# The causal mask of the mLSTM gates: on GpSimd after the exponential instead of in a matmul before it

## The chip, the cores and the metric

The kernel runs on one core of a Trainium2 chip. The metric is the device time of one execution in microseconds (us). The engines of the core are named PE (TensorE, matmuls; PEld is its weight load), DVE (VectorE), ACT (ScalarE), POOL (GpSimd) and SP (SyncE, here a DMA queue). SBUF is the on-chip memory in which tiles lie, PSUM the banks into which PE writes.

## The reference, cut to what matters

The model is a trunk of two layers over 256 tokens of width 1024. Each layer has a half-step SwiGLU network, a mixer, and a second half-step SwiGLU network, with a normalization before and after each. The mixer projects the tokens, runs differential attention on four heads and an mLSTM on four other heads beside it, and projects both back. The change is in the mLSTM, whose gates make a causal matrix of weights in each chunk:

```
causal = jnp.tril(jnp.ones((CHUNK, CHUNK), dtype=bool))
D = jnp.where(causal, b[..., :, None] - b[..., None, :] + log_i[..., None, :], -jnp.inf)
m_inter = b + m_prev[..., None]
m = jnp.maximum(m_inter, D.max(-1))
w = jnp.exp(D - m[..., None]) * jnp.einsum('bhcjd,bhcsd->bhcjs', q, k)
```

For a query j and a key s of the same chunk the exponential is exp(D - m), at most one where s <= j, and zero where s > j. Everywhere above the diagonal the unmasked exponent can be of any size. The kernel works with chunks of 128 tokens, so that its chunk is one tile of tokens, and keeps the matrix turned round: keys on the 128 partitions, four heads of 128 queries in the 512 columns.

## The kernel before, in words

The weights come from HBM in pieces of 1 MB on SP's queue (`begin_piece`, L281). Each half of a piece is split in two parts for accuracy: ACT rounds it to the PE's fast float32 form (tile wh, L287), DVE subtracts that from the original (wl, L288). A product of the activations xh, xl with such weights is three matmuls of 128x512 (`mm3`, L401 to L403: xh by wh, xh by wl, xl by wh). The feed-forward networks take most of the time and use the same split (L611, L614).

The mixer projects two tiles of 128 tokens (t = 0, 1) through six groups of 512 columns. Its order of work is written by hand: `traverse` lists steps of one `mm3` each, and `AT` (L39) gives for every stage of the rest the step in front of which it stands. PE follows that order exactly; for ACT, DVE and POOL the framework fixes an order when the program is built, from the dependencies, from priorities and from its own estimate of when operands are there. Every engine then runs its queue in that order. The projections go to two PSUM banks in turn (tag pin), and an evacuation on ACT frees them: `rope` (L1056) for queries and keys, `values_ml` (L1151), `output_gate`.

The stages that matter here, by the step in front of which they stand:

- 22, `gate_chain`: the running sums of the gates and their maximum on DVE, in rows (tiles ul and md).
- 24, `conv_input_t(1)`, `conv((2, 3))`, `gate_exps(0)`, `gate_exps(1)` and `roped(0, 0)`. `gate_exps(t)` multiplies ul by md on PE (L997), which spreads u[s] - M[j] over a 128x512 bank, adds the mask in the same bank by a second matmul (L998: the identity by the mask, 0 where allowed and -1e30 elsewhere), and takes the exponential on ACT into the tile eE (the helper `func`, L265).
- 40, `conv((0, 1))`, and 46, `conv_silu`: the causal convolution of the mLSTM's queries and keys, each block one step on ACT (L906) and three on DVE (L909), and its SiLU on ACT (tile qk).
- 34, 43, 57, `roped`: transposes on PE (L878) of the rotated queries and keys of the attention. The rotation itself is four DVE instructions in `rope` (L1057, twice L1062, L1063), made for each token tile when its projection is done.
- 52, `scores` and `intra_weights`: the attention scores, and the product of eE with the mLSTM's scores on DVE (L1048, tile wt).
- 60 and later, `combine`, `normed_ml`, `attend`: here POOL computes reciprocal square roots as powers (`rsqrt`, L416). Besides these, POOL sets memory at the start (L218 to L248) and copies four small gate tiles in each layer (L943).

The mask, the rounded mask and the rounded identity are made once, in `constants_mix` (L201 to L206), in the middle of the first network.

Of the kernel before, what the change touches and what calls it, by code (L numbers as in the profile page):

```python
# [17 lines left out]
F32 = mybir.dt.float32  # L18
F32R = mybir.dt.float32r
AF = mybir.ActivationFunctionType  # L20
ALU = mybir.AluOpType
# [3 lines left out]
P = 128  # L25
# [7 lines left out]
CH = P  # L33
EPS = 1e-6
BIG = -1.0e30
# [23 lines left out]
def _pack(inp):  # L59


    f32 = np.float32
    x = np.asarray(inp["x"])
    w_in, w_out = np.asarray(inp["ffn_w_in"]), np.asarray(inp["ffn_w_out"])
    m_in, m_out = np.asarray(inp["mix_w_in"]), np.asarray(inp["mix_w_out"])
    g = np.asarray(inp["norm_gains"])
    w = np.empty((L * PIECES_LAYER, P, 2048), f32)

    def ffn(at, l, f):
        a = w_in[l, f].reshape(2, 4, P, 2, NC_FF, 256)  # L70
        a = a.transpose(4, 0, 2, 1, 3, 5).reshape(NC_FF, 2, P, 2048)
        b = w_out[l, f].reshape(NC_FF, 2, P, D).transpose(0, 2, 1, 3).reshape(NC_FF, P, 2048)
        order = [a[0, 0], a[0, 1]]
        for c in range(1, NC_FF):
            order += [a[c, 0], a[c, 1], b[c - 1]]
        for piece in order + [b[NC_FF - 1]]:
            w[at] = piece
            at += 1

    for l in range(L):  # L80
        at = l * PIECES_LAYER
        ffn(at, l, 0)
        at += PIECES_FFN
        for n, lo in enumerate(MIX_GROUPS):
            a = m_in[l][:, lo:lo + 512].reshape(2, 4, P, 512).transpose(0, 2, 1, 3)
            w[at + 2 * n:at + 2 * n + 2] = a.reshape(2, P, 2048)
        at += 2 * len(MIX_GROUPS)
        w[at:at + 4] = m_out[l].reshape(4, 2, P, D).transpose(0, 2, 1, 3).reshape(4, P, 2048)
        ffn(at + 4, l, 1)
    for i in range(2):  # L90
        w[i] = w[i].reshape(P, 4, 512).transpose(1, 0, 2).reshape(P, 2048)

    arrays = {
        "x": x.reshape(NT, P, 2, 512).transpose(0, 2, 1, 3),
        "w": w,
        "gpost": g[:, 1::2].reshape(L * 3, D),
        "lam": np.asarray(inp["da_lambda"]).reshape(L, 256),
    }
    arrays = {k: np.ascontiguousarray(v) for k, v in arrays.items()}
    gpre = g[:, 0::2].reshape(L, 3, KT, P).transpose(3, 0, 1, 2).reshape(P, L * 3 * KT)  # L100
    arrays["c0"] = np.concatenate([np.eye(P, dtype=f32), gpre], 1)

    inv = (f32(10000.0) ** (-np.arange(0, 64, 2, dtype=f32) / f32(64))).astype(f32)
    ang = np.arange(S, dtype=f32)[:, None] * inv[None, :]
    cos, sin = np.cos(ang).astype(f32), np.sin(ang).astype(f32)
    rope = np.stack([np.concatenate([cos, cos], 1), np.concatenate([-sin, sin], 1)])
    s = np.arange(P)[:, None]
    j = np.arange(P)[None, :]
    mask = np.where((s // CH == j // CH) & (s <= j), 0.0, BIG).astype(f32)
    first = (np.arange(S) % CH == 0)  # L110
    scan = np.stack([np.where(first, 0.0, 1.0), np.where(first, BIG, 0.0)]).astype(f32)

    def everywhere(v):
        return np.broadcast_to(np.asarray(v).reshape(1, -1), (P, np.asarray(v).size))

    parts = {
        "wg": m_in[:, :, 3072:3080].reshape(L, KT, P, 8).transpose(2, 0, 1, 3),
        "rope": rope.reshape(2, NT, P, 64).transpose(2, 0, 1, 3),
        "convw": np.asarray(inp["ml_conv_w"]).reshape(L, 4, 4, P).transpose(3, 0, 2, 1),
        "convb": np.asarray(inp["ml_conv_b"]).reshape(L, 4, P).transpose(2, 0, 1),  # L120
        "gda": np.asarray(inp["da_subln_g"]).T,
        "gml": np.asarray(inp["ml_norm_g"]).T,
        "gateb": everywhere(inp["ml_gate_b"]),
    }
    arrays["c1"] = np.concatenate([parts[n].reshape(P, -1) for n, _ in C1], 1)
    arrays["mask"] = mask
    arrays["scan"] = np.ascontiguousarray(np.broadcast_to(scan.reshape(1, 512), (100, 512)))
    return arrays


class _Trunk:
# [50 lines left out]
    def constants_mix(self):  # L182
        nc, a = self.nc, self.a
# [11 lines left out]
        for l in range(L):  # L195
# [2 lines left out]
        self.wgc = self.const.tile([P, L, KT, 16], F32R, name="c_wgc")  # L198
        ia = nc.scalar.activation(self.wgc[:, :, :, 0:8], self.wg, AF.Copy)
        iv = nc.vector.tensor_tensor(self.wgc[:, :, :, 8:16], self.wg, self.wgc[:, :, :, 0:8].bitcast(F32), op=ALU.subtract)  # L200
        mraw = self.t2("mraw", (P, P))  # L201
        self.after(nc.sync.dma_start(mraw, a["mask"]), [self.load])
        self.mask = self.const.tile([P, P], F32R, name="c_mask")
        self.identr = self.const.tile([P, P], F32R, name="c_identr")
        nc.scalar.activation(self.mask, mraw, AF.Copy)
        self.after(nc.scalar.activation(self.identr, self.ident, AF.Copy), [ia])  # L206

        lamv = self.t2("lamv", (P, L, 4, 64))
        self.after(nc.sync.dma_start(lamv.rearrange("p l a b -> p l (a b)"), a["lam"].partition_broadcast(P)), [self.load])
# [11 lines left out]
                                     op=ALU.add)  # L221
# [535 lines left out]
class _Mixer:  # L757
# [234 lines left out]
    def gate_exps(self, t):  # L992

        tr = self.tr
        cols = slice(t * P, t * P + P)
        pe = tr.bank_bk()
        self.mm(pe, tr.ul[:, cols], tr.md[:, t].rearrange("p h j -> p (h j)"), start=True, stop=False)  # L997
        self.mm(pe, tr.identr, tr.mask.unsqueeze(1).broadcast_to([P, 4, P]), start=False, stop=True)  # L998
        eE = tr.t2("eE")
        tr.func(eE, pe, AF.Exp)  # L1000
        self.eE.append(eE)

    def gate_decays(self):
# [252 lines left out]
```

## Time and profile before

| what | us |
|---|---|
| median of the runs | 977.39 (977.36 to 977.74) |
| the profiled execution | 979.73 |
| its span | 976.9 |
| busy: PE, DVE, ACT, POOL | 969.4, 710.2, 568.0, 30.1 |
| granted clock of PE, mean | 0.999 |

The profile records one execution. The span runs from the first to the last instruction of the program; the execution's time has 2.8 us more around it. A line of the profile gives the line of the kernel, the engine, the operation, and the tiles as out<-in without their numbers; L265 and L416 are helpers, so there one goes by the tiles. The busy time of PE counts matmuls that overlap, and their ends are modelled. "Idle before" is the time that an engine stood still just before an instruction, with the instruction that ended it.

### The profile page before, as it was taken

The numbers are of one execution on the slowest core, as the hardware profiler recorded it, in microseconds if no ns is written. First come the engines' busy times: TensorE is split into PE (matmuls) and PEld (weight loads), VectorE is DVE, ScalarE is ACT, GpSimd is POOL, SyncE is SP. The second block draws the span as 40 slices with busy tenths as digits, with TensorE's granted clock in tenths as the row PEclk, the third lists the DMA queues.
The fourth block names the chain that finished last, engine by engine and source line by source line (L and its number), as shares of the span: only waits on it lengthen the run. The fifth ranks groups of instructions, "written<-read, shape, count | busy, mean of one in ns | idle before, by whom it ended". The sixth has DMA issues, their size and how long they took to land.

```text
span 976.9 us, 13520 instructions
## 1 busy us (share of the span) xinstructions
PE 969.4 (99%) x5061; PEld 818.1 (84%) x5061; DVE 710.2 (73%) x1178; ACT 568.0 (58%) x1041; POOL 30.1 (3%) x55
## 2 busy tenths in 40 slices
PE   9999999999999999999999999999999999999997
PEld 6888888888788888888888888888888888888886
DVE  6787676689867677767687767676997687776664
ACT  7665554477756565455375545454778475555541
POOL 2000000000020000000000000000001000000000
PEclk9999999999999999999999999999999999999999
DMA  8954545336352845564356456443454256554511
GB/s 296 353 199 174 206 170 198 142 129 225 118 197 92 317 163 182 180 240 183 131 204 233 151 205 221 174 171 114 173 209 172 88 207 239 202 193 173 193 67 43
DMA packets 27647, 178.92 MB, mean 183 GB/s; under 512 B 3034, under 2 KB 4186, under 8 KB 6846
## 3 DMA queue, kind: packets, MB, share of 16 engines
q1 hardware_dynamic: 27006, 177.46, 50.0%
q8 instruction: 39, 0.64, 0.3%
q10 hardware_dynamic: 576, 0.61, 0.2%
q14 instruction: 26, 0.21, 0.1%
HBM read 177.01 MB, written 1.05 MB: 182 GB/s over the span
## 4 chain that ended last, share of the span: by engine, by line
PE 99%; DVE 0%; ACT 0%; POOLq 0%; issue 0%; DVEq 0%; ACTq 0%
PE ptr L611 14%; PE pin L611 14%; PE bk L402 10%; PE bk L403 10%; PE bk L401 10%; PE pin L401 7%; PE pin L403 7%; PE pin L402 7%; PE ptr L614 7%; PE pin L614 7%; PE ptr L878 1%; PE ptr L427 1%; PE bk L1093 1%; PE bk L1131 1%; PE bk L378 0%; PE bk L379 0%
## 5 line engine op out<-in xcount | busy, mean ns | idle before, releaser
L288 DVE TENSOR_TENSOR wl<-wr,wh 128x1024 fp32r<-128x1024 f32 x324 | 388.6, 1222 | 130.3 <-ACT wh L287 128.5
L287 ACT ACTIVATE wh<-wr 128x1024 fp32r<-128x1024 f32 x324 | 332.1, 1053 | 123.8 <-PE ptr L611 57.7
L611 PE MATMUL pin<-both,wh 128*128 128x512 f32 x576 | 157.3, 394 | 0.0
L611 PE MATMUL ptr<-both,wh 128*128 128x512 f32 x576 | 157.0, 394 | 0.0
L402 PE MATMUL bk<-wl,hh 128*128 128x512 f32 x352 | 137.6, 391 | 0.0
L401 PE MATMUL bk<-wh,hh 128*128 128x512 f32 x352 | 137.4, 390 | 0.0
L403 PE MATMUL bk<-wh,hl 128*128 128x512 f32 x352 | 136.8, 391 | 0.0
L401 PE MATMUL pin<-wh,both 128*128 128x512 f32 x304 | 122.3, 403 | 0.0
L402 PE MATMUL pin<-wl,both 128*128 128x512 f32 x304 | 118.9, 392 | 0.0
L403 PE MATMUL pin<-wh,both 128*128 128x512 f32 x304 | 118.7, 391 | 0.0
L611 PEld LDWEIGHTS pin<-both,wh 128*128 128x128 f32 x576 | 100.7, 189 | 14.9
L611 PEld LDWEIGHTS ptr<-both,wh 128*128 128x128 f32 x576 | 98.8, 189 | 13.8
L614 PEld LDWEIGHTS ptr<-both,wl 128*128 128x128 f32 x576 | 88.3, 189 | 12.2
L614 PEld LDWEIGHTS pin<-both,wl 128*128 128x128 f32 x576 | 88.2, 189 | 11.7
L614 PE MATMUL pin<-both,wl 128*128 128x256 f32 x576 | 92.4, 281 | 0.0
L614 PE MATMUL ptr<-both,wl 128*128 128x256 f32 x576 | 91.6, 281 | 0.0
L546 ACT ACTIVATE hh<-su 128x256 fp32r<-128x256 f32 (+1 forms) x96 | 32.1, 355 | 94.4 <-PE bk L402 77.9
L403 PEld LDWEIGHTS bk<-wh,hl 128*128 128x128 f32 x352 | 66.1, 188 | 14.0
L401 PEld LDWEIGHTS bk<-wh,hh 128*128 128x128 f32 x352 | 66.1, 188 | 12.8
L402 PEld LDWEIGHTS bk<-wl,hh 128*128 128x128 f32 x352 | 66.1, 188 | 12.8
L403 PEld LDWEIGHTS pin<-wh,both 128*128 128x128 f32 x304 | 57.1, 188 | 12.4
L401 PEld LDWEIGHTS pin<-wh,both 128*128 128x128 f32 x304 | 57.2, 188 | 11.8 <-issue 0.7
(203 smaller groups left out, 982.9 us busy)
## 6 DMA issues: line engine op xcount, KB each, us to landing
wr<-in_w_dram SPq DMA_DIRECT2D x162, 1024.0 KB, 4.8
gpost<-in_gpost_dram SPq DMA_DIRECT2D x6, 512.0 KB, 5.7
wr<-in_w_dram SPq DMA_DIRECT2D x2, 512.0 KB, 6.0
wr<-in_w_dram SPq DMA_DIRECT2D x3, 256.0 KB, 4.2
x<-in_x_dram SPq DMA_DIRECT2D x3, 256.0 KB, 4.8
out_dram<-x SPq DMA_DIRECT2D x2, 256.0 KB, 2.1
x<-in_x_dram SPq DMA_DIRECT2D x2, 128.0 KB, 3.0
wr<-in_w_dram ACTq DMA_DIRECT2D x1, 256.0 KB, 3.9
```

The source lines that it names most:

```text
L287: ia = nc.scalar.activation(hi, raw[:, j], AF.Copy)
L288: iv = nc.vector.tensor_tensor(lo, raw[:, j], hi.bitcast(F32), op=ALU.subtract)
L401: mm(ps, xh, wh, start=start, stop=False)
L402: mm(ps, xh, wl, start=False, stop=False)
L403: mm(ps, xl, wh, start=False, stop=stop)
L427: nc.tensor.transpose(ptr[:, k, :], x[:, (4 * hf + k) * P:(4 * hf + k + 1) * P], self.ident)
L546: self.nc.scalar.activation(hh, h, AF.Copy)
L611: self.nc.tensor.matmul(b, self.cols(w, k)[0][:, c], both[:, k].rearrange("p i t -> p (i t)"), start=kh == 0 and k == 0, stop=False, skip_ ...
L614: self.nc.tensor.matmul(b[:, 0:NT * P], self.cols(w, k)[1][:, c], both[:, k, 0:NT].rearrange("p i t -> p (i t)"), start=False, stop=kh == ...
L878: self.T(ptr[:, b, :], a[:, b * P:(b + 1) * P], self.tr.ident)
L1093: self.mm(pcs[c][:, h, :], self.qkT[0][rows, h0 + h, t * P:(t + 1) * P], self.qkT[1][rows, h0 + h, 0:nk], start=True, stop=True)
L1131: self.mm(po[:, h, :], self.aT[t][:, kt, h, :], self.vd[:, kt, h * P:(h + 1) * P], start=kt == 0, stop=kt == t)
```

## The change

The mask changes from 0 and -1e30 to 1 and 0. `gate_exps` loses the second matmul. After the exponential, two instructions on POOL work in place on eE: a minimum with one, which bounds what lies above the diagonal, and a product with the mask, repeated over the four heads. The rounded identity and the two rounding copies on ACT go; the mask is loaded straight into its constant tile.

```
@@ in _pack
-    mask = np.where((s // CH == j // CH) & (s <= j), 0.0, BIG).astype(f32)
+    mask = np.where(s <= j, 1.0, 0.0).astype(f32)
@@ in constants_mix
-        mraw = self.t2("mraw", (P, P))
-        self.after(nc.sync.dma_start(mraw, a["mask"]), [self.load])
-        self.mask = self.const.tile([P, P], F32R, name="c_mask")
-        self.identr = self.const.tile([P, P], F32R, name="c_identr")
-        nc.scalar.activation(self.mask, mraw, AF.Copy)
-        self.after(nc.scalar.activation(self.identr, self.ident, AF.Copy), [ia])
+        self.mask = self.const.tile([P, P], F32, name="c_mask")
+        self.after(nc.sync.dma_start(self.mask, a["mask"]), [self.load])
@@ in gate_exps
-        self.mm(pe, tr.ul[:, cols], tr.md[:, t].rearrange("p h j -> p (h j)"), start=True, stop=False)
-        self.mm(pe, tr.identr, tr.mask.unsqueeze(1).broadcast_to([P, 4, P]), start=False, stop=True)
+        self.mm(pe, tr.ul[:, cols], tr.md[:, t].rearrange("p h j -> p (h j)"), start=True, stop=True)
         eE = tr.t2("eE")
         tr.func(eE, pe, AF.Exp)
+        e4 = eE.rearrange("p (h j) -> p h j", h=4)
+        tr.nc.gpsimd.tensor_scalar(eE, eE, 1.0, None, op0=ALU.min)
+        tr.nc.gpsimd.tensor_tensor(e4, e4, tr.mask.unsqueeze(1).broadcast_to([P, 4, P]), op=ALU.mult)
         self.eE.append(eE)
```

## The prediction

> **What bounds the kernel now.** I read the page first: the busy shares and the chain that ended last. Then the waits of TensorE (PE) alone.
>
> ```profile
> PE 969.4 (99%) x5061; PEld 818.1 (84%) x5061; DVE 710.2 (73%) x1178; ACT 568.0 (58%) x1041; POOL 30.1 (3%) x55
> PE 99%; DVE 0%; ACT 0%; POOLq 0%; issue 0%; DVEq 0%; ACTq 0%
> ```
>
> ```profile
> PE bk L390 <- DVE mp L979: 1.2, 1, 1.2
> ```
>
> PE is busy for 99% of the span, the chain is PE from end to end, and the only wait of PE that the trace lists is one of 1.2 us at the very start. So the time is the sum of what PE issues. Two kinds of change count: one that takes instructions off PE, and one that makes PE wait where it never waited. VectorE (DVE) at 73% as an average says nothing yet; it has to be read in the stage that the change touches.
>
> **What a matmul of the mask is worth.** The timeline of PE around the edited lines, second layer (columns: start, busy time, engine, line, operation, tiles), and the group of the removed line over the whole span (last numbers: busy us in total, mean ns of one, idle us before):
>
> ```profile
> 704.50 0.47 PE L997 MATMUL bk<-md,ul 100*128 100x512 f32 x1
> 704.82 0.40 PE L998 MATMUL bk<-c_mask,c_identr 128*128 128x512 f32 x1
> 705.05 0.39 PE L997 MATMUL bk<-md,ul 100*128 100x512 f32 x1
> 705.28 0.40 PE L998 MATMUL bk<-c_mask,c_identr 128*128 128x512 f32 x1
> 705.52 0.60 PE L878 MATMUL ptr<-c,ra 128*128 128x128 f32 x4
> ```
>
> ```profile
> L998 PE MATMUL bk<-c_mask,c_identr 128*128 128x512 f32 x4 | 1.6, 396 | 0.0
> ```
>
> The group says 396 ns each, 1.6 us in all, but matmuls overlap: what one costs is the distance to the next start. L998 starts at 704.82 and 705.28, its followers at 705.05 and 705.52: 0.23 and 0.24, 0.47 us for the two of a layer. Two layers make 0.93 us, 0.1% of the time. Its weight loads lie beside other matmuls and go at nothing. The two ScalarE (ACT) copies of the set-up, L205 and L206, go too; they run once, off PE's chain, and I price them at nothing. The mask's DMA stays. The exponential keeps its size.
>
> **What GpSimd (POOL) is given.** For each of two token tiles in each of two layers, a minimum (one input, 128x512) and a product (two inputs, 128x512). The trace has no arithmetic of that size on POOL. Its nearest rows, with mean ns of one after the bar:
>
> ```profile
> L218 POOL MEMSET g<- 128x512 f32 x1 | 0.5, 524 | 0.0
> L240 POOL MEMSET vx<- 128x1032 f32 x1 | 1.0, 963 | 0.0
> L943 POOL COPY g<-gn 128x16 f32<-128x16 f32 x4 | 0.7, 202 | 14.8 <-DVE gn L941 14.8
> L416 POOL TENSOR_TENSOR rs<-s,c_half 128x1 f32<-128x1 f32 x24 | 13.1, 552 | 767.9 <-DVE s L452 767.9
> ```
>
> The memsets give (963-524)/520 = 0.84 ns per column, the small copy about 0.20 us of fixed cost. The minimum is then an estimated 0.20+0.43 = 0.63 us, and the product, which has to fetch two operands, 0.20+2x0.43 = 1.06 us: 1.69 us a tile, 3.4 us a layer. A lower bound is the plain memset, 0.52 each.
>
> In time POOL has room. The exponentials (ACT timeline, first layer) and the first reader of the masked tile (DVE timeline):
>
> ```profile
> 223.70 0.59 ACT L265 ACTIVATE eE<-bk 128x512 f32<-128x512 f32 x1
> 226.15 0.58 ACT L265 ACTIVATE eE<-bk 128x512 f32<-128x512 f32 x1
> ```
>
> ```profile
> 248.87 0.73 DVE L1048 SCALAR_TENSOR_TENSOR wt<-bk,eE 128x256 f32<-128x256 f32 x2
> ```
>
> The tiles are there at 224.29 and 226.73 and are wanted at 248.87: 22 us for 3.4 us of work. L1048 now waits for POOL instead of ACT; behind it in DVE's queue stand the maxima of the attention scores.
>
> **What POOL does to VectorE.** This is where the sum turns. POOL's powers beside DVE's instructions, first layer, POOL's timeline and then DVE's:
>
> ```profile
> 270.14 1.01 POOL L416 TENSOR_TENSOR rs<-ssm,c_half 128x4 f32<-128x4 f32 x1 [61.91 <-ACT wh L287]
> 271.56 1.01 POOL L416 TENSOR_TENSOR rs<-ssa,c_half 128x4 f32<-128x4 f32 x1 [0.41 <-DVE ssa L1138]
> 273.52 2.09 POOL L416 TENSOR_TENSOR rs<-ssa,c_half 128x4 f32<-128x4 f32 x1 [0.94 <-DVE ssa L1138]
> 278.84 1.28 POOL L416 TENSOR_TENSOR rs<-ssm,c_half 128x4 f32<-128x4 f32 x1 [3.23 <-DVE ssm L1205]
> ```
>
> ```profile
> 270.18 1.23 DVE L288 TENSOR_TENSOR wl<-wr,wh 128x1024 fp32r<-128x1024 f32 x1 [0.19 <-ACT wh L287]
> 273.52 1.23 DVE L288 TENSOR_TENSOR wl<-wr,wh 128x1024 fp32r<-128x1024 f32 x1
> 278.58 0.69 DVE L1189 SCALAR_TENSOR_TENSOR so<-so,hn 128x512 f32<-128x512 f32 x1
> ```
>
> These rows settle two things on the way. POOL's queue is empty until 270.14, so nothing of its own waits behind the new instructions. And the far end of POOL's price: a power of 128x4 takes 1.01 us against 0.55 for 128x1, 0.15 us per column, which would be 79 us for 512. I stay with the memset's pace, since the copy of 16 columns at 0.20 us is nowhere near the power's.
>
> Now the port. The same power takes 1.01 us twice, but 2.09 when L288, a DVE instruction with two SBUF inputs, starts with it, and 1.28 beside L1189, which also has two. Taking 1.01 off the ends 275.61 and 280.12, POOL got going at 274.60 and 279.11; the DVE instructions end at 274.75 and 279.27. So POOL stood still until 0.15 us before their end: the two exclude each other. The trace doesn't show the reverse, DVE held by POOL; beside the power at 270.14, L288 keeps its 1.23 us, though that power reads four columns only. Now DVE in the stretch where the new instructions fall: first the stretches view (columns: window, length, busy time of PE, PEld, DVE, ACT, POOL with counts, granted clock, DMA), then DVE's timeline.
>
> ```profile
> 224.00:237.30 13.30, 13.30 (x64) 11.07 (x63) 13.30 (x26) 12.62 (x17) 0.00 (x0) 1.00 0.62 232
> ```
>
> ```profile
> 224.21 0.68 DVE L1057 TENSOR_TENSOR ra<-rv,c 128x512 f32<-128x512 f32 x1
> 224.81 0.75 DVE L1062 TENSOR_TENSOR rb<-rv,c 128x256 f32<-128x256 f32 x2
> ...
> 227.22 4.44 DVE L909 SCALAR_TENSOR_TENSOR conv<-xpad,c,conv 128x256 f32<-128x256 f32 x11
> ...
> 236.65 0.69 DVE L1063 TENSOR_TENSOR ra<-ra,rb 128x512 f32<-128x512 f32 x1
> ```
>
> DVE is busy for 13.30 of 13.30 us, and each of those instructions (rotation, convolution, weight split) reads two SBUF tensors. So whatever POOL takes from DVE between 224.3 and 236.7 comes out late at 236.65, with nothing to absorb it. Does POOL get in? In back-to-back work DVE's next instruction starts 0.08 us before the end of the one before (224.81 against 224.21+0.68); POOL got going 0.15 us before. It was there first, so I take it that POOL wins at the next boundary and DVE then stands still while POOL reads.
>
> **Who waits for DVE there.** The rotated keys of L1063 are transposed on PE by L878 (PE's timeline, then the second layer's pair from DVE and PE):
>
> ```profile
> 237.83 0.60 PE L878 MATMUL ptr<-c,ra 128*128 128x128 f32 x4
> ```
>
> ```profile
> 718.23 0.69 DVE L1063 TENSOR_TENSOR ra<-ra,rb 128x512 f32<-128x512 f32 x1
> ```
>
> ```profile
> 719.41 0.60 PE L878 MATMUL ptr<-c,ra 128*128 128x128 f32 x4
> ```
>
> L1063 ends at 237.34 and 718.92, the transposes start at 237.83 and 719.41: 0.49 us of slack in both layers. Removing the two L998 brings PE there 0.47 us earlier, while DVE, which is behind, comes no earlier. So the change of a layer is the larger of -0.47 and d-0.49, with d the time that DVE loses: the gain is spent as soon as d reaches 0.49. A second path is nearly as tight:
>
> ```profile
> 233.22 1.06 ACT L265 ACTIVATE qk<-conv 128x1024 f32<-128x1024 f32 x1 [0.28 <-DVE conv L909]
> 234.19 0.67 ACT L1056 ACTIVATE rv<-pin,rs 128x512 f32<-128x512 f32 x1
> ```
>
> ```profile
> 235.78 0.39 PE L401 MATMUL pin<-wh,both 128*128 128x512 f32 x1
> ```
>
> ACT's SiLU waits for the convolution on DVE; behind it in ACT's queue, L1056 empties the bank that PE refills at 235.78 (the second token tile of the values): 234.86 against 235.78, slack 0.92, 0.45 with PE earlier. It would show a stall first; the transposes then add the rest, so the two aren't added up.
>
> **The sum.** d lies between nothing (POOL yields always) and 3.4 us (DVE loses all of POOL's time); without POOL's fixed 0.20 of each instruction, when it reads nothing, 2.6. I take 3.0, between the last two. Each layer then loses 3.0-0.49 = 2.5 us, two lose 5.0. The profiled execution took 979.73 us with a span of 976.9; it would take 984.7 with a span of 981.9. It lies 2.34 above the median of the runs, 977.39; the difference carries over, so the median becomes 982.4.
>
> The Trainium skill bears on two of these places. "SBUF — State Buffer", section "Who interferes with whom", says that a DVE instruction with two SBUF inputs and a GpSimd instruction that reads SBUF hold the shared port against each other, the first for its whole instruction; the trace agrees on DVE holding off POOL (2.09 against 1.01), but the whole instruction is too much for a power of four columns, beside which L288 kept its 1.23. "GPSIMD Engine Reference", section 3.1, gives 4497 ns for an addition of two tensors of 2048 columns and 769 ns for a tight loop over 512: an estimated 1.12+0.77 a tile, so d = 3.8 and a loss of 6.6 instead of 5.0; no row here has either.
>
> **The rivals.** *POOL yields* (not slower): POOL gets no boundary while DVE runs back to back. It works in DVE's pauses before 248.87, and PE keeps its 0.93: 976.5. For it: the trace has no DVE instruction lengthened by POOL. Against it: the 0.15 us by which POOL was first, twice. It decides from d under 0.49. Chance 0.28.
>
> *A partial hold*: POOL stops DVE only while it actually fetches, or DVE reaches the rotation in another order, so that d is between 0.49 and 1.47. Then two layers cost up to 2x(1.47-0.49) = 1.96, which is the 0.2%: 976.5 to 979.3. Chance 0.08.
>
> *The mask comes late*: if POOL computes at the power's pace, the tile isn't ready at 248.87, L1048 stands in DVE's queue and with it the scores. At 79 us an instruction, 316 us a layer less the 24.6 from 224.29 to 248.87: some 580 us more for both. For it only that pow row, against it the copy's. Chance 0.02.
>
> Forecast 0.62: the cases of d from 1.47 to 4.5, that is 979.3 to 985.4.
>
> **How the numbers follow.** 0.2%, 1.95 us, is about what a measurement of this kernel can tell from no change. Slower: 0.62+0.02 = 0.64. Same: the -0.93 of a yielding POOL is within it, and so is the partial hold: 0.28+0.08 = 0.36, of which I set 0.03 aside as faster, for a reordering of DVE that I can't see; on PE there is no more than 0.93 to be had. The range starts at 976.4, so that it holds the yielding POOL, and ends at 985.2, which is d = 4.4: POOL a third slower than the memset's pace makes it. The forecast's own range is 979.3 to 985.2.
>
> **What would show it.** Right: L998 gone; two pairs of POOL instructions of about 0.6 and 1.1 us or longer after each exponential; DVE instructions there that start late or last 0.5 to 1.1 us longer; the waits of PE, empty so far, naming L1063 before L878, or L1056's bank before L401, some 2.5 us a layer; all other stages of the same length. Wrong: PE's waits still empty and the span 0.9 shorter (POOL yields); or the stall elsewhere, at L1048 and the scores (the mask late); or POOL's instructions far from 0.6 and 1.1 without a wait.

## The result and the profile after

The changed kernel takes 989.05 us (median of 4 runs, 988.13 to 990.87) against 977.38 us before: a ratio of 1.012 (95% interval 1.0108 to 1.0132), 11.7 us slower. The forecast was 982.4 us, 5.0 slower. The direction held, and the wait came where it was expected, but it was longer and brought a second cost behind it.

The page of the changed kernel, its busy shares, the granted clock in 40 slices and the chain that ended last (lines move by 4 to 2 against before: L1061 is the old L1063, L874 the old L878, L284 the old L288, L905 the old L909):

```profile
span 989.1 us, 13523 instructions
PE 973.5 (98%) x5057; PEld 820.0 (83%) x5057; DVE 716.1 (72%) x1178; ACT 567.0 (57%) x1039; POOL 43.5 (4%) x63
PEclk9999999998999999999999999999989999999999
PE 94%; DVE 4%; issue 0%; ACT 0%; DMA 0%; POOLq 0%; DVEq 0%; ACTq 0%
```

PE has lost its four matmuls, and DVE has entered the chain with 4%. Two slices of the clock, one in each layer's mixer, show an 8 where all stood at 9. The waits of PE (us in total, times, longest):

```profile
PE ptr L874 <- DVE ra L1061: 8.1, 2, 4.0
```

Twice 4.0 us, at the transposes of the rotated keys, one wait in each layer. PE's timeline of the first layer's place, with the four instructions behind the wait:

```profile
236.55 0.39 PE L399 MATMUL pin<-wh,both 128*128 128x512 f32 x1
240.97 1.09 PE L874 MATMUL ptr<-c,ra 128*128 128x128 f32 x4 [4.03 <-DVE ra L1061]
241.71 0.78 PE L397 MATMUL pin<-wh,both 128*128 128x512 f32 x1
242.28 0.63 PE L398 MATMUL pin<-wl,both 128*128 128x512 f32 x1
242.71 0.63 PE L399 MATMUL pin<-wh,both 128*128 128x512 f32 x1
```

Behind the wait matmuls start 0.43 us apart instead of 0.23. The stretches view shows why (window, length, busy PE, PEld, DVE, ACT, POOL, then the granted clock; the last two columns are DMA):

```profile
241.50:246.50 5.00, 5.00 (x15) 3.99 (x14) 3.56 (x5) 1.65 (x2) 0.00 (x0) 0.51 0.81 295
246.50:252.00 5.50, 5.50 (x42) 4.52 (x42) 2.06 (x4) 2.82 (x4) 0.00 (x0) 1.00 0.15 63
729.50:734.50 5.00, 5.00 (x15) 3.94 (x14) 3.45 (x5) 1.65 (x2) 0.00 (x0) 0.50 0.74 279
```

For about 5 us after the wait PE runs at half its clock, in both layers of the profiled execution. Set against the trace of before, matmul by matmul, the distance of PE's starts changes, behind the start-up, in three places of each layer alone. In the first layer it stands at -0.61 us before the gates (the start-up, which varies from run to run), goes to -1.08 where the mask matmuls are missing, to 3.14 at the transposes and to 5.69 in the half-clock stretch. In the second it goes from 5.69 to 5.23, 9.45 and 12.11. Each layer so loses 4.2 us to the wait and 2.6 to the clock, and gains 0.47: 6.3 to 6.4, twice.

Now the two engines that share the place. POOL's new groups and DVE's timeline, first layer:

```profile
L997 POOL TENSOR_SCALAR eE<-eE 128x512 f32<-128x512 f32 x4 | 8.2, 2056 | 32.4 <-ACT eE L261 32.4
L998 POOL TENSOR_TENSOR eE<-eE,c_mask 128x512 f32<-128x512 f32 x4 | 5.5, 1385 | 0.0
```

```profile
223.61 0.69 DVE L1055 TENSOR_TENSOR ra<-rv,c 128x512 f32<-128x512 f32 x1
224.21 1.17 DVE L1060 TENSOR_TENSOR rb<-rv,c 128x256 f32<-128x256 f32 x2
...
227.45 5.77 DVE L905 SCALAR_TENSOR_TENSOR conv<-xpad,c,conv 128x256 f32<-128x256 f32 x9
...
237.88 2.35 DVE L284 TENSOR_TENSOR wl<-wr,wh 128x1024 fp32r<-128x1024 f32 x2
240.15 0.68 DVE L1061 TENSOR_TENSOR ra<-ra,rb 128x512 f32<-128x512 f32 x1
```

From the first of these instructions to the end of the key rotation DVE took 13.13 us before (224.21 to 237.34); now it takes 17.22 (223.61 to 240.83). Two things are in that. Instructions are longer: the pair of L1060 lasts 1.17 instead of 0.75. And the order is another: ahead of the rotation's last step stand two weight splits in a row, where one stood before:

```profile
235.51 1.22 DVE L288 TENSOR_TENSOR wl<-wr,wh 128x1024 fp32r<-128x1024 f32 x1
```

The framework fixed a new order when the program was built. ACT's queue shows a new order too: both exponentials now stand in a row, ahead of the four convolution steps that stood between them before (223.70 and 226.15 in the prediction):

```profile
223.09 1.08 ACT L261 ACTIVATE eE<-bk 128x512 f32<-128x512 f32 x2
```

That the framework does this because the second exponential is ready one matmul earlier is argued, not shown; for it speaks that e3, which puts the convolution steps back between the two, brings back DVE's order.

### The profile page after: what moved, and what is told of

Read it like the earlier page. It is cut to its first block, busy times and chain, and to the rows that moved or that the text cites. A ratio compares the mean times of both kernels' runs of the same rounds, so it can differ in the third digit from the quotient of the medians.

```text
span 989.1 us, 13523 instructions
## 1 busy us (share of the span) xinstructions
PE 973.5 (98%) x5057; PEld 820.0 (83%) x5057; DVE 716.1 (72%) x1178; ACT 567.0 (57%) x1039; POOL 43.5 (4%) x63
## 4 chain that ended last, share of the span: by engine, by line
PE 94%; DVE 4%; issue 0%; ACT 0%; DMA 0%; POOLq 0%; DVEq 0%; ACTq 0%
PE ptr L607 14%; PE pin L607 13%; PE bk L398 10%; PE bk L399 10%; PE bk L397 10%; PE ptr L610 7%; PE pin L610 7%; PE pin L397 6%; PE pin L398 6%; PE pin L399 6%; DVE wl L284 2%; DVE conv L905 1%; PE ptr L423 1%; PE ptr L874 1%; PE bk L1091 1%; PE bk L1129 1%
## 5 line engine op out<-in xcount | busy, mean ns | idle before, releaser
L284 DVE TENSOR_TENSOR wl<-wr,wh 128x1024 fp32r<-128x1024 f32 x324 | 388.5, 1222 | 131.4 <-ACT wh L283 129.8
L397 PE MATMUL pin<-wh,both 128*128 128x512 f32 x304 | 124.4, 410 | 0.0
L399 PE MATMUL pin<-wh,both 128*128 128x512 f32 x304 | 120.2, 396 | 0.0
L610 PEld LDWEIGHTS pin<-both,wl 128*128 128x128 f32 x576 | 88.2, 189 | 11.7
L397 PEld LDWEIGHTS bk<-wh,hh 128*128 128x128 f32 x352 | 66.1, 188 | 12.8
L398 PEld LDWEIGHTS bk<-wl,hh 128*128 128x128 f32 x352 | 66.1, 188 | 12.8
L399 PEld LDWEIGHTS pin<-wh,both 128*128 128x128 f32 x304 | 58.2, 192 | 12.8
L397 PEld LDWEIGHTS pin<-wh,both 128*128 128x128 f32 x304 | 58.4, 192 | 12.2 <-issue 0.7
```

The lines of the kernel that those rows point to most:

```text
L284: iv = nc.vector.tensor_tensor(lo, raw[:, j], hi.bitcast(F32), op=ALU.subtract)
L397: mm(ps, xh, wh, start=start, stop=False)
L398: mm(ps, xh, wl, start=False, stop=False)
L399: mm(ps, xl, wh, start=False, stop=stop)
L610: self.nc.tensor.matmul(b[:, 0:NT * P], self.cols(w, k)[1][:, c], both[:, k, 0:NT].rearrange("p i t -> p (i t)"), start=False, stop=kh == ...
```

## The experiments

Three theories. The first: POOL's reading holds DVE for about 3 us a layer, and the new order adds one split. The second: the new order alone. The third, about the rest: PE's clock drops after a long enough wait, and that costs as much again as the forecast's whole loss. e1 to e4 ran on one chip with the kernel before beside them (977.75 us there), e5 to e8 on another (977.46).

**e1: without POOL.** The two instructions go, and the masking with them; the new order stays.

```
-        tr.nc.gpsimd.tensor_scalar(eE, eE, 1.0, None, op0=ALU.min)
-        tr.nc.gpsimd.tensor_tensor(e4, e4, tr.mask.unsqueeze(1).broadcast_to([P, 4, P]), op=ALU.mult)
```

> The changed kernel without its two GpSimd instructions; the masking is left out. VectorE keeps the queue order of the changed kernel, in which one more weight split (1.14 us) stands ahead of the key rotation than before. Theory 1 (GpSimd's reading holds VectorE for about 2.95 us a layer, the new order adds 1.14): the rotation is late by 1.14 against 0.49 of slack, a net loss of 0.65 a layer, about 978.7, and more (up to 984) if the PE clock drops after a wait of only 1.1 us. Theory 2 (the new order alone makes the loss): about 989, as the changed kernel. Theory 3 (no order effect, GpSimd alone): 976.5.

979.2 us, ratio 1.0015 (1.0006 to 1.0024). PE's wait, and DVE where it was long (timeline):

```profile
PE ptr L874 <- DVE ra L1059: 2.1, 2, 1.1
```

```profile
224.28 0.68 DVE L1053 TENSOR_TENSOR ra<-rv,c 128x512 f32<-128x512 f32 x1
224.88 0.75 DVE L1058 TENSOR_TENSOR rb<-rv,c 128x256 f32<-128x256 f32 x2
...
227.29 3.65 DVE L905 SCALAR_TENSOR_TENSOR conv<-xpad,c,conv 128x256 f32<-128x256 f32 x9
...
235.59 2.35 DVE L284 TENSOR_TENSOR wl<-wr,wh 128x1024 fp32r<-128x1024 f32 x2
237.86 0.69 DVE L1059 TENSOR_TENSOR ra<-ra,rb 128x512 f32<-128x512 f32 x1
```

No instruction is lengthened, and the stretch takes 14.27 us: 1.14 more than before, one weight split. So the order alone turns a saving into a loss: it makes the rotation 1.14 later in each layer, PE waits 1.06, and the clock stays full. The second theory falls: the order makes 1.5 us of the 11.7, with the missing matmuls in it. And 17.22-14.27 = 2.95 us a layer is what POOL takes from DVE.

**e2: the kernel before, plus POOL.** The mask matmul and the old order stay; after each exponential POOL does a minimum in place (there without effect) and a product of the same size into a scratch tile, with the identity in the place of the mask.

```
         tr.func(eE, pe, AF.Exp)
+        e4 = eE.rearrange("p (h j) -> p h j", h=4)
+        tr.nc.gpsimd.tensor_scalar(eE, eE, 1.0, None, op0=ALU.min)
+        tr.nc.gpsimd.tensor_tensor(tr.junk_tile().rearrange("p (h j) -> p h j", h=4), e4,
+                                   tr.ident.unsqueeze(1).broadcast_to([P, 4, P]), op=ALU.mult)
```

> The kernel before, mask matmul and VectorE order unchanged, plus the minimum in place (without effect there) and a product of the same size into a scratch tile on GpSimd after each exponential. Theory 1: VectorE loses about 2.95 us a layer, PE waits 2.95-0.49 = 2.5 us in each, and the half clock after it costs about 2.5 more: 987. Without a clock effect: 982.3. Theory 2: 977.4, since the order is that of before.

983.25 us, ratio 1.0055 (1.0039 to 1.0072): 5.5 us, near the 982.3 that stood there for the case without a clock effect, and not the 987 with one. The waits of PE, and a stretch behind the second layer's:

```profile
PE pin L401 <- ACT rv L1059: 3.8, 2, 1.9
PE ptr L878 <- DVE ra L1066: 0.5, 2, 0.2
```

```profile
723.00:729.00 6.00, 5.77 (x28) 4.54 (x27) 5.89 (x9) 3.78 (x5) 0.00 (x0) 1.00 0.64 209
```

With the old order the hold shows on the second path of the prediction, the bank that ACT empties behind the SiLU, and the transposes add the rest: 1.9 and 0.2 us. In the change that path is gone, since ACT empties the bank at 232.19, ahead of the SiLU at 237.99. Over both waits PE's starts fall back by 2.6 us a layer. The clock stays full: the second cost doesn't follow every wait.

**e3: the change, in the old order.** The ScalarE steps of the convolution are put ahead of the second exponential, which gives DVE back the order of before.

```
-            lambda: self.conv((2, 3)),
+            lambda: self.conv((2, 3, 0, 1)),
...
-            lambda: self.conv((0, 1)),
+            lambda: None,
...
-            self.act(conv[:, b, :], ...
+            self.conv_act = self.act(conv[:, b, :], ...
...
-        tr.func(eE, pe, AF.Exp)
+        i = tr.func(eE, pe, AF.Exp)
+        if t == 1:
+            tr.after(i, [self.conv_act])
```

> The changed kernel with VectorE's queue in the order of before (the convolution's ScalarE steps ahead of the second exponential). Theory 1: the hold of 2.95 is left and 1.14 of order goes: a PE wait of about 2.9 instead of 4.0 a layer, and about 2.3 us less in all: 986 to 987. Theory 2: 976.5. If the clock stays full after the shorter wait: 982.

985.05 us, ratio 1.0076 (1.0061 to 1.0091), between the two cases. PE's wait, DVE's lengthened instructions, and the clock behind the wait in the first and the second layer:

```profile
PE ptr L874 <- DVE ra L1063: 5.7, 2, 2.9
```

```profile
224.33 1.17 DVE L1062 TENSOR_TENSOR rb<-rv,c 128x256 f32<-128x256 f32 x2
...
226.56 1.77 DVE L1063 TENSOR_TENSOR ra<-ra,rb 128x512 f32<-128x512 f32 x1
228.25 5.86 DVE L905 SCALAR_TENSOR_TENSOR conv<-xpad,c,conv 128x256 f32<-128x256 f32 x11
```

```profile
240.00:245.00 5.00, 5.00 (x25) 4.21 (x26) 5.00 (x7) 2.41 (x4) 0.00 (x0) 1.00 0.73 242
725.00:730.00 5.00, 5.00 (x13) 3.93 (x13) 4.21 (x5) 1.65 (x2) 0.00 (x0) 0.50 0.71 269
```

The hold can be read instruction by instruction against before: 1.17 for 0.75 while the first minimum reads (+0.42), 1.77 for 0.69 at the first product (+1.08), 5.86 for 4.44 at the second pair (+1.42): 2.9 us. The wait of 2.87 us is the same in both layers, but in the profiled execution the clock dropped at one of them only, and the time lies accordingly: 5.7 of waits, less the 0.9 gained, and 2.6 for one half-clock stretch make 7.4, against 7.3 by the medians. (By the starts' distance the profiled execution, at 986.18 the slowest of the four, lost 8.0.)

**e4: PE kept busy.** The changed kernel, with matmuls that nobody needs in the place of the wait.

```
+        if (i, t) == (1, 0):
+            spare = self.tr.bank_bk()
+            for _ in range(18):
+                self.mm(spare, self.tr.ul[:, 0:P], self.tr.md[:, 0].rearrange("p h j -> p (h j)"), start=True, stop=True)
```

> The changed kernel with 18 spare matmuls (the gate matmul again, into a bank that nobody reads; 18 times 0.227 is 4.1 us) on PE ahead of the key transposes, where PE waits 4.0 us. If the half clock after the wait is part of the loss (2.5 us a layer): the transposes start when they did, the clock stays at 1.0, and the time falls by about 5 to 984. If the clock is not a cause: 989 as before.

984.89 us, ratio 1.0074 (1.0059 to 1.0089): the loss is 7.1 us instead of 11.7, so 4.5 go, by adding work. The stretch that ran at half clock, now:

```profile
241.50:246.50 5.00, 5.00 (x27) 4.21 (x26) 3.27 (x6) 2.58 (x3) 0.00 (x0) 1.00 0.76 285
```

27 matmuls where 15 went through in the same five microseconds. The rotation is as late as it was; only the clock differs. So the clock is a cause of its own, shown with everything else left in place.

**e5: old order, no POOL.** e3 without its two POOL instructions.

> The changed kernel without its two GpSimd instructions and with VectorE's order of before; the masking is left out. It has nothing of the change but the missing mask matmuls. Theory 1 (hold plus order): the rotation is ready 0.02 us before PE comes, so PE waits at most for the way of the signal, under 0.1 us a layer, and the time is 0.7 to 0.9 below before: a ratio of 0.9991 to 0.9993. If something else in the change costs time, it isn't below before.

976.69 us, ratio 0.9990 (0.9981 to 0.9999): 0.8 us below before. That is what the missing matmuls are worth here, and it is less than the 0.93 that the starts' distance gave. The list of PE's waits names none in the mixer, but the starts show a short one: PE is 0.47 us early before the transposes of a layer and 0.34 to 0.36 behind them. DVE's rotation ends at 235.79 and the transposes start at 235.94; the same 0.14 to 0.15 us lie between the two in e1 (238.55 to 238.69) and in the change (240.83 to 240.97).

**e6: POOL writes, and doesn't read.** e3 with four memsets per tile in place of minimum and product.

```
-        tr.nc.gpsimd.tensor_scalar(eE, eE, 1.0, None, op0=ALU.min)
-        tr.nc.gpsimd.tensor_tensor(e4, e4, tr.mask.unsqueeze(1).broadcast_to([P, 4, P]), op=ALU.mult)
+        for _ in range(4):
+            tr.nc.gpsimd.memset(eE, 0.5)
```

> As e3 (changed kernel, VectorE's order of before), but each tile gets four memsets of 0.52 us on GpSimd in place of minimum and product: the same engine busy at the same place for some 2.1 us a tile, writing the same tile and reading nothing; the masking is left out. If what holds VectorE is GpSimd's reading: no VectorE instruction is lengthened, PE doesn't wait, time as e5, about 976.8. If any work of GpSimd holds VectorE: about 2 us a layer of hold, PE waits 1.5 to 2 a layer, 980 to 981.

976.54 us, ratio 0.9989 (0.9980 to 0.9998), as e5. POOL's and DVE's timelines:

```profile
222.84 1.11 POOL L999 MEMSET eE<- 128x512 f32 x2 [16.12 <-ACT eE L261]
224.01 1.11 POOL L1001 MEMSET eE<- 128x512 f32 x2
225.28 1.11 POOL L999 MEMSET eE<- 128x512 f32 x2 [0.16 <-ACT eE L261]
226.45 1.11 POOL L1001 MEMSET eE<- 128x512 f32 x2
```

```profile
223.29 0.76 DVE L1063 TENSOR_TENSOR rb<-rv,c 128x256 f32<-128x256 f32 x2
225.70 4.44 DVE L905 SCALAR_TENSOR_TENSOR conv<-xpad,c,conv 128x256 f32<-128x256 f32 x11
```

POOL is busy for 4.4 us beside the same DVE instructions, and neither is longer than alone. So it is not any work of POOL that holds DVE: instructions that read SBUF do, memsets, which only write it, don't. A memset differs from minimum and product in its operation too; no run here reads without computing.

**e7: the mask after the rotation.** The change in the old order, POOL's part moved to a stage of its own, behind a copy of one column of the last rotation.

```
+    def gate_mask(self):
+        tr, pool = self.tr, self.tr.nc.gpsimd
+        i = pool.tensor_copy(tr.small("gate", (P, 1)), self.rot[3][:, 0:1])
+        for eE in self.eE:
+            e4 = eE.rearrange("p (h j) -> p h j", h=4)
+            tr.after(pool.tensor_scalar(eE, eE, 1.0, None, op0=ALU.min), [i])
+            pool.tensor_tensor(e4, e4, tr.mask.unsqueeze(1).broadcast_to([P, 4, P]), op=ALU.mult)
```

> The whole change with VectorE's order of before, and GpSimd's minimum and product put behind the last rotation (a copy of one column of it on GpSimd comes first), 241.5 instead of 224 us in the first layer, when the first reader comes at 249. Theory 1: GpSimd reads where VectorE has pauses and one-input work; no PE wait at the key transposes, 0.7 to 0.9 below before, 976.5 to 977. Rival: the hold moves to the weight splits and the scores, the mask is late at 249 and PE waits at the transposes of the scores, up to 2 us a layer: 979 to 980.

979.08 us, ratio 1.0014 (1.0005 to 1.0023). The rival was right about the time and the late mask. PE's wait, POOL, and DVE's two weight splits there with the readers of the mask:

```profile
PE ptr L1129 <- DVE p L1127: 1.5, 2, 0.8
```

```profile
241.57 3.99 POOL L1006 TENSOR_SCALAR eE<-eE 128x512 f32<-128x512 f32 x2
245.53 3.57 POOL L1007 TENSOR_TENSOR eE<-eE,c_mask 128x512 f32<-128x512 f32 x2
```

```profile
243.00 1.22 DVE L284 TENSOR_TENSOR wl<-wr,wh 128x1024 fp32r<-128x1024 f32 x1
245.46 1.23 DVE L284 TENSOR_TENSOR wl<-wr,wh 128x1024 fp32r<-128x1024 f32 x1 [0.22 <-ACT wh L283]
247.88 0.42 DVE L1054 SCALAR_TENSOR_TENSOR wt<-bk,eE 128x256 f32<-128x256 f32 x1 [0.34 <-POOL eE L1007]
249.13 0.42 DVE L1054 SCALAR_TENSOR_TENSOR wt<-bk,eE 128x256 f32<-128x256 f32 x1 [0.83 <-POOL eE L1007]
```

Here POOL takes 7.6 us for the two tiles, its rows taken with all that they wait for, and the mask is late. The hold didn't move to the weight splits, as the rival had it: they keep their 1.22 us, and POOL waits instead. Its second minimum and first product, which fall on a split, take 2.50 and 2.32 us, the other two 1.52 and 1.30 (single records, which the timeline adds up). DVE stands for 0.34 and 0.83 us, the scores behind it come late, and PE waits 0.75 at their transposes.

**e8: the mask on DVE.** As e7, with one DVE instruction per tile and POOL idle.

```
+        for eE in self.eE:
+            e4 = eE.rearrange("p (h j) -> p h j", h=4)
+            tr.after(self.stt(e4, e4, 1.0, tr.mask.unsqueeze(1).broadcast_to([P, 4, P]), op0=ALU.min, op1=ALU.mult), [self.turned])
```

> As e7, but minimum and product are one VectorE instruction per tile, 0.7 us, behind the last rotation, and GpSimd does nothing. Theory 1: VectorE has 0.84 and 0.76 us of pauses behind it, which take most of the 1.4 us; no PE wait: 976.5 to 977. If the scores come late by the rest: up to 978.

976.61 us, ratio 0.9990 (0.9981 to 0.9999): below both kernels, though by 0.8 us only. DVE's timeline has the two instructions:

```profile
239.75 1.29 DVE L1005 SCALAR_TENSOR_TENSOR eE<-eE,c_mask 128x512 f32<-128x512 f32 x2
```

1.29 us a layer on an engine that is busier than POOL, but at a place where it has a pause behind it. The list of PE's waits names none in the mixer.

## Why the prediction was right in direction and short in size

- **PE's gain.** 0.47 a layer, priced by the starts' distance and not by the 396 ns of the group: seen as 0.47 and 0.46 in the trace of the change. Of the 0.93 us for both layers e5 keeps 0.8; the transposes take the rest.
- **That POOL gets in.** The forecast rested on POOL getting going 0.15 us before a DVE instruction's end. It got in at each boundary where DVE's two-input instructions stood back to back (the change, e2, e3), and "POOL yields" fell. e6 adds that it needs POOL to read, and e7 that it needs such work back to back: beside single weight splits POOL waited.
- **The hold d.** Taken as 3.0 us a layer; measured 2.95 (after against e1) and 2.9 (e3 against before). The parts were 0.42 for a minimum and 1.08 for a product; the memset's pace had given 0.43 and 0.86 without the fixed cost. The 3.0 was set between two sums, 2.6 and 3.4, and neither was right in its parts, so that it fell this close is partly luck.
- **POOL's own rows.** Expected about 0.6 and 1.1 us or longer; they show 2.06 and 1.39. They hold POOL's waits for DVE too (in e7 a minimum took 1.52 and 2.50, a product 1.30 and 2.32), so a POOL row beside a busy DVE isn't a price.
- **The order, first failed step.** "whatever POOL takes from DVE between 224.3 and 236.7 comes out late at 236.65, with nothing to absorb it" took DVE's order as given, and so put what a new order costs at nothing. The edit without POOL's instructions moves a weight split ahead of the rotation: 1.14 us a layer more (e1). The prediction named another order only as a way to less loss.
- **The size of a wait, second failed step.** "Each layer then loses 3.0-0.49 = 2.5 us" priced a wait of PE at its length. The wait became 4.0, and behind it came half the clock for 5 us: 2.6 us a layer. e4 takes this term away alone and 4.5 us go.
- **The slack, a smaller one.** "0.49 us of slack in both layers" counted to the start of the transposes and left out the 0.14 us that pass between the rotation's end and that start. So 0.35 us were free. e1 lost 0.8 a layer by the starts' distance, which is 1.14-0.35, and e2 lost 2.6, which is 2.95-0.35; e5 could gain no more than 0.35.
- **The sum.** Forecast 5.0. With the order, 2x1.14 = 2.3, the clock, 2x2.6 = 5.2, and the slack, 2x0.14 = 0.3, it makes 12.8; the trace has 12.7 for the two layers, the medians 11.7. Between runs of the changed kernel the time differs by 2.7 us, with mean clocks of 0.992 to 0.996: the half-clock stretches aren't equally long each time. That last link is argued from these clocks, not tried.
- **The range** ended at 985.2, above e3 (985.05) and e4 (984.89), from which one of the two missing terms each is taken away, and below the change, which has both: it widened d and held neither term.
- **The rivals.** The mask was never late in the change: POOL is done at 230.6, the reader comes at 254.6. It was late in e7, from POOL starting 18 us later, not from the power's pace.

## What to carry to other kernels

A matmul that is taken off a PE that never waits is worth its distance to the next start; a wait that takes its place costs its length and, if it is long enough (here 4.0 us, and 2.87 once of two), a stretch of half clock behind it, so the two must be priced apart. Before work goes to an idle GpSimd, look at what VectorE does at that moment: if it runs instructions with two SBUF inputs back to back, GpSimd's reads come out of VectorE's time, and the question is who waits for VectorE within the next microseconds. And compare the engines' order before and after any edit, even one that only removes: here the removal alone moved a weight split in front of the one step that had little time to spare.

## What the runs showed of the hardware beyond what was expected

- PE's granted clock fell to 0.50 for about 5 us after waits of 4.0 us (both layers of the changed kernel); after waits of 1.06 (e1) and 1.9 us (e2) it stayed at 1.00; after 2.87 us (e3) it fell in one layer and not in the other. "TensorE: Matmul & The Clock Gate" of the Trainium skill, Part 1, has the clock drop to half after an idle window of about 3.4 us that runs freely, and rise again after a busy one. That 2.87 us falls on both sides agrees with a free-running window; that it can be enough is below the page's figure, and the measurement decides. The times of the drops show more (stretches view, the change and then e3):

```profile
236.94:239.60 2.66, 0.00 (x0) 0.00 (x0) 2.66 (x5) 1.60 (x2) 0.00 (x0) 1.00 0.60 253
239.60:246.43 6.83, 5.46 (x15) 4.52 (x16) 5.46 (x8) 3.45 (x4) 0.00 (x0) 0.50 0.75 254
721.21:723.29 2.08, 0.00 (x1) 0.00 (x0) 2.08 (x5) 2.07 (x3) 0.00 (x0) 1.00 0.95 398
723.29:730.11 6.82, 6.03 (x17) 4.91 (x18) 5.92 (x9) 2.56 (x3) 0.00 (x0) 0.50 0.67 228
```

The clock falls while PE still waits and stays at half for 6.83 us, of which 5.5 lie behind the wait in the change. Its four changes there (239.60, 246.43, 727.71, 734.53) are 2, 141 and 2 times 3.413 us apart. Counted in the same steps, such a moment lies 2.08 us into the second wait of e3, where the clock fell, and 1.53 into the first, where it didn't. That a drop needs some 2 idle us before such a moment is worked out from these times and tried by no run.
- POOL's reads of 128x512 held DVE for 0.42 us with one input and 1.08 with two; POOL's writes (memsets of 128x512, 0.53 us each) held it for nothing. "SBUF — State Buffer" of the Trainium skill, "Who interferes with whom", says that reads contend with VectorE's two-input instructions and writes don't. It also says, in its line on VectorE's two-port modes, that the first comer holds the ports for its whole instruction; here the hold is shorter than POOL's instruction, which took 1.52 us (minimum) and 1.30 (product) in e7 where no two-input instruction of DVE stood in its way.
- How much waiting a POOL row can hold: in e7 the copy of one column ahead of the mask (at 240.49) is recorded with 1.12 us, beside a weight split that had begun 0.15 us before it; a copy of 16 columns took 0.20 us in the kernel before.
